# Attention probabilities times values as three rounded-half products in a fused decoder layer

## The chip, the cores and the metric

The kernel runs on one core of one Trainium2 chip. The metric is device time in microseconds (us) of one execution. The engines are TensorE (PE in the profile; PEld is its weight load), VectorE (DVE), ScalarE (ACT), GpSimd (POOL) and SyncE (SP), which issues the loads.

## What is computed

One layer of a hybrid decoder over 256 tokens of width 1024: a normalised input `h` goes through one wide input projection, three parallel branches (a matrix memory with four heads, a convolution module, native sparse attention) are computed from it, gated and merged, and an output projection follows. The change lies in the attention. Eight query heads share two groups of keys and values. For each head there are three softmaxes: over compressed keys (`kc`, 15 of them), over selected blocks, and over a window; at this length the last two cover all earlier tokens.

```python
s_c = jnp.einsum('bqgjd,bngd->bgjqn', qb, kc).astype(jnp.float32) * scale
p_c = masked_softmax(s_c, cmp_end[None, :] <= t[:, None])
o_c = jnp.einsum('bgjqn,bngd->bqgjd', p_c.astype(vc.dtype), vc)
...
o_s = jnp.einsum('bgjqk,bgqkd->bqgjd', p_s.astype(vs.dtype), vs)
...
o_w = jnp.einsum('bgjqk,bkgd->bqgjd', p_w.astype(vw.dtype), vw)
return gb[..., 0:1] * o_c + gb[..., 1:2] * o_s + gb[..., 2:3] * o_w
```

## The kernel before

All weights are streamed from HBM once, in tiles of 128 x 1024 (`w_raw`). Each is split in two: ACT casts it to the rounded format (`w_hi`, float32r), DVE subtracts to get the rest (`w_lo`), and a product with the likewise split `h` is the sum of three rounded-half matmuls (`feat`, L548; `group_feat`, L560; results in the PSUM tiles `ps_f`, and `ps_t` for token-major ones). One 128-wide output tile of `ps_f` is 24 matmuls of 256 columns.

A small planner, the `Loom` (L67 to L243), fixes the order of all instructions when the program is built. Every PE, ACT and DVE instruction goes through it; it estimates when each ends, and side work, written as generators that yield the time at which their operands should be due, is stepped between the matmuls of the projection (`weave`, L199, called in `feat`). Filler, the 31-tap convolution (`conv_gen`, L607, instructions named `acc`), is stepped whenever DVE looks idle. `need(task)` (L225) ends the waiting: it steps a generator to its end at once, and what is left of it is then issued in one block, with no projection matmul in between.

The attention is one such generator, `nsa_gen` (L898). It goes through four groups (two key groups g, two halves t of the tokens). For each: score products into `ps_s`, masks and maxima on DVE (`mx`), 12 exponentials on ACT over the tile `pm`, normalisation on DVE, and then per block of 128 keys: four transposes (`flip`) of `pm` into a PSUM bank `ps_p`, an ACT copy to `p_t`, and one f32 matmul of 512 columns with the values `vtok`, accumulated in `ps_o`. The compressed keys are one more block, of 16 rows, through `ptc` and `vcmp`. A group with t = 0 has two dense blocks, one with t = 1 has four; each has one compressed block. PSUM tag `sd` has three banks: one for `ps_o`, two for `ps_p`.

Around it, the program issues the projection groups in this order: four heads of `aq`, `ak`, `av`, `az`, `bz`; then `ao` (eight tiles, L1180), evacuated by ACT with a Sigmoid into `sz`; then `need(g_nsa)` (L1182), since the next group, `cz`, multiplies into the attention's output `oc`. Later three branch products follow (`ps_br`): c, then a, then b. Branch b needs the end of the convolution, a layer norm (`lnorm_gen`, L618: `ps_mu`, `ps_rc`), and `conf_tail` (L665): Silu on ACT, product with `zb` on DVE, split into `yb_hi` (ACT) and `yb_lo` (DVE). Its gates `gb` are projected just before, eight tiles, and then `need(g)` (L1245) forces what is left of `conf_tail`. Within a branch tile the products go pair by pair through the eight tiles of `y` in order.

Of the kernel before, what the change touches and what calls it, by code (L numbers as in the profile page):

```python
# [11 lines left out]
F32 = mybir.dt.float32  # L12
F32R = mybir.dt.float32r
# [51 lines left out]


class Loom:  # L67
    """Issues the instructions of every engine in the order of the trace and estimates when each one ends, so that
    side work can be woven between the matrix products once its operands are due."""

    HOP = {"pe": 250.0, "act": 130.0, "dve": 150.0, "dma": 0.0}
    OWN = {"pe": 0.0, "act": 140.0, "dve": 125.0, "dma": 0.0}
# [68 lines left out]
        return end  # L141

    def clocked(self, start, cost):
        """The tensor engine runs at half its clock after a window in which it was mostly idle."""
        w = int(start // 3413)
        while self.window < w:
            self.cold = self.busy < (0.9 if self.cold else 0.5) * 3413
            self.busy = 0.0
            self.window += 1
        self.busy += cost * (2 if self.cold else 1)  # L150
        return cost * (2 if self.cold else 1)
# [64 lines left out]
                self.tasks.remove(task)  # L216

    def spawn(self, gen, rank=2):
        """Ranks: 0 for what the tensor engine needs next, 1 for the chains of the heads, 2 for the rest."""
        task = [0.0, gen, False, rank]  # L220
        i = next((i for i, t in enumerate(self.tasks) if t[3] > rank or (t[3] == rank == 1)), len(self.tasks))
        self.tasks.insert(i, task)
        return task
# [5 lines left out]
        self.forcing -= 1  # L229

    def calm(self, engine, ap):
        """Waits while a run of exponentials keeps its table loaded."""
        yield self.until(engine, ap)
        while self.run and not self.forcing:
            yield self.now() + 300
# [8 lines left out]


class Line:
    """An engine whose instructions go through a Loom."""

    def __init__(self, loom, engine, name):
        self.loom, self.engine, self.name = loom, engine, name  # L250
# [7 lines left out]
def trunk(ctx: ExitStack, tc, xtok, crow, wada, wave0, wgrp, wmisc, w1, wbr, wout, par, vbias, out):  # L258
# [24 lines left out]
    def ringt(pool_, shape, name, tag, bufs, dt=F32):  # L283
        return loom.alloc(pool_.tile(shape, dt, name=name, tag=tag, bufs=bufs), tag, bufs)
# [431 lines left out]
    ckv = ckb[:, 0].rearrange("p (a b c) -> p a b c", a=2, b=2)  # L716
    kk = [const.tile([128, 528], F32, name=f"kk{g}") for g in range(2)]
    vtok = midt("vtok", [128, 2, 2, 256])
    vcmp = [const.tile([128, 128], F32, name=f"vcmp{g}") for g in range(2)]
    for g in range(2):  # L720
        pool.memset(vcmp[g], 0.0)

    def cmp_gen(j):
        for g in range(2):
            c = ckv[:, j, g, :]
            src = bass.AP(tensor=c.tensor, offset=c.offset, ap=[list(c.ap[0]), [1, 32], [16, 15]])
            dve.tensor_tensor(blk[:, :, 16 * g:16 * g + 15], src,
                              pc("pe", 32 * j, 32)[:, :, None].broadcast_to([128, 32, 15]), op=OP.add)
        yield from loom.slot("sd")
        ps = bank("ps_c1", "sd")  # L730

        def load(c):
            w = rawt([128, 8, 256], "w1_raw")
            loom.load(nc.sync, w, w1[4 * j + c])
            return w

        yield from raw_slot()
        nxt = load(0)
        for c in range(4):
            if c < 3:  # L740
                yield from raw_slot()
            w, nxt = nxt, load(c + 1) if c < 3 else None
            yield until("pe", w, blk)
            for e in range(8):
                q = e % 4
                mm(ps[32 * q:32 * q + 32, 0:256], blk[:, 8 * c + e, :], w[:, e], c == 0 and e < 4,
                   c == 3 and e >= 4, tile_position=(0, 32 * q), skip_group_check=True)
            raw_free(w)
        part = ringt(work, [128, 256], "part", "mu", 1)
        yield until("act", ps)  # L750
        act.copy(part, ps[:, 0:256])
        drop(ps)
        yield until("pe", part)
        yield from loom.slot("sd")
        ps = bank("ps_c2", "sd")
        for f in range(2):
            mm(ps[:, 32 * f:32 * f + 32], part[:, 128 * f:128 * f + 128], gather4, True, True)
        hid = work.tile([128, 64], F32, name="hid", tag="hid")
        yield until("act", ps)
        act.copy(hid, ps[:, 0:64])  # L760
        drop(ps)
        yield until("dve", hid)
        t = work.tile([128, 64], F32, name="gt", tag="gt")
        dve.tensor_tensor(t, hid, hid, op=OP.mult)
        dve.tensor_tensor(t, t, hid, op=OP.mult)
        dve.scalar_tensor_tensor(t, t, 0.044715, hid, op0=OP.mult, op1=OP.add)
        yield until("act", t)
        act.activation(t, t, AF.Tanh, scale=0.7978845608028654)
        yield until("dve", t)
        dve.tensor_scalar(t, t, 0.5, 0.5, op0=OP.mult, op1=OP.add)  # L770
        dve.tensor_tensor(hid, hid, t, op=OP.mult)
        yield until("pe", hid)
        w2 = [pc("w2", (2 * j + f) * 128, 128) for f in range(2)]
        if j == 0:
            yield from loom.slot("sd")
            ps = bank("ps_kc", "sd")
            for f in range(2):
                mm(ps[:, 0:32], w2[f], hid[:, 32 * f:32 * f + 32], f == 0, f == 1)
            yield until("act", ps)
            for g in range(2):  # L780
                act.copy(kk[g][:, 384:400], ps[:, 16 * g:16 * g + 16])
            drop(ps)
        else:
            for g in range(2):
                yield from loom.slot("sd")
                ps = bank("ps_vc", "sd")
                for f in range(2):
                    mm(ps[0:16, 0:128], hid[:, 32 * f + 16 * g:32 * f + 16 * g + 16], w2[f], f == 0, f == 1)
                yield until("act", ps)
                act.copy(vcmp[g][0:16, :], ps[0:16, 0:128])  # L790
                drop(ps)

    blk = ckb[:, 1].rearrange("p (a b) -> p a b", a=32)
# [104 lines left out]
    def nsa_gen(qs, oc, ptc):  # L898
        for g in range(2):
            for t in range(2):  # L900
# [80 lines left out]
                def flips(c, kind, kt):  # L981
# [4 lines left out]
                        flip(pt[0:w, 128 * j:128 * j + 128], pm[:, j, c:c + w])  # L986
                    yield until("act", pt)
                    if kind == 2:
                        act.copy(ptc[0:16, :], pt[0:16, :])
                        drop(pt)  # L990
                        return vcmp[g], ptc
                    p_t = ringt(work, [128, 512], "p_t", "p_t", 2)
                    act.copy(p_t, pt)
                    drop(pt)
                    return vtok[:, kt, kind, 128 * g:128 * g + 128], p_t

                ops = yield from flips(*blocks[0])
                for b in range(len(blocks)):
                    v, p_t = ops
                    if b + 1 < len(blocks):  # L1000
                        ops = yield from flips(*blocks[b + 1])
                    yield until("pe", p_t)
                    mm(po, v, p_t, b == 0, b == len(blocks) - 1)
                yield until("act", po)
                act.copy(oc[:, 4 * g:4 * g + 4, 128 * t:128 * t + 128], po.rearrange("p (j q) -> p j q", j=4))
                drop(po)
# [101 lines left out]
    for i in range(4):  # L1108
        group_feat("cq", i, evac_fn(lambda t: qs[:, t]))
    oc = bigt("oc")  # L1110
    ptc = const.tile([128, 512], F32, name="ptc")
    pool.memset(ptc, 0.0)

    def nsa_all():
        yield from loom.after(g_cmp, g_misc)
        yield from nsa_gen(qs, oc, ptc)

# [306 lines left out]
```

## Time and profile before

| | |
|---|---|
| runs (us) | 512.29, 512.80, 513.61; median 512.8 |
| profiled execution, span | 510.6 us; the median of the runs is 2.2 above it |
| PE busy | 502.0 us (98%), 3962 matmul instructions |
| PEld busy | 476.6 us (93%) |
| DVE busy | 431.5 us (85%), 894 instructions |
| ACT busy | 316.9 us (62%), 542 instructions, 27 of them table loads |
| DMA | 103.86 MB, mean 203 GB/s |
| chain that ended last | PE 96% |

The profiled execution has no time of its own beside its span, so the runs' median is what it is held against. A matmul's length in the time line includes its pipeline; the chain of waits shows how long each took from TensorE alone, from one start to the next. An f32 matmul shows as two instructions. On ACT a table load (ACT_TABLE_LOAD) precedes a function of another table than the last: Exp, Sigmoid, Silu and Sqrt each have their own here; copies, casts and Identity need none.

### The profile page before, as it was taken

What the parts mean: (1) busy time and instruction counts of PE and PEld (TensorE: products, weight loads), DVE (VectorE), ACT (ScalarE), POOL (GpSimd) and SP (SyncE); (2) the same over time, 40 slices, a digit from 0 to 9 for tenths busy, and PEclk for the clock granted to TensorE, in tenths of its full rate; (3) what the DMA queues carried; (4) which work ended last, traced back from release to release, by engine and by line L of the source; (5) the groups of instructions that cost most, each with busy time, mean ns of one, the idle gap of its engine ahead of it and who ended that gap; (6) DMA issues with size and microseconds to landing.
All of it is one profiled execution on the core that took longest, in us unless ns stands there. A gap on an engine that the chain in (4) does not pass through costs nothing.

```text
span 510.6 us, 10012 instructions
## 1 busy us (share of the span) xinstructions
PE 502.0 (98%) x3962; PEld 476.6 (93%) x3962; DVE 431.5 (85%) x894; ACT 316.9 (62%) x542; POOL 7.5 (1%) x42
## 2 busy tenths in 40 slices
PE   8999999999999999999999999999999999999994
PEld 6999999899889989979999989999999999999983
DVE  4998888899987998988989968999899997667755
ACT  5556666244566867779568995665534466975442
POOL 4000000000000000000000000000000000000000
PEclk9999999999999999999999999999999999999999
DMA  7999975884694424422523415544675664445502
GB/s 263 380 367 367 421 236 189 292 323 167 223 358 163 164 83 166 143 105 90 190 119 134 162 60 210 197 166 171 243 282 213 235 254 172 166 166 198 214 1 82
DMA packets 17617, 103.86 MB, mean 203 GB/s; under 512 B 2081, under 2 KB 2209, under 8 KB 7458
## 3 DMA queue, kind: packets, MB, share of 16 engines
q1 hardware_dynamic: 17570, 103.22, 55.0%
q8 instruction: 31, 0.51, 0.4%
q14 instruction: 16, 0.13, 0.1%
HBM read 102.16 MB, written 1.05 MB: 202 GB/s over the span
## 4 chain that ended last, share of the span: by engine, by line
PE 96%; DMA 1%; DVE 1%; ACT 0%; issue 0%; DVEq 0%; SPq 0%; ACTq 0%
PE ps_f L158 50%; PE ps_br L158 14%; PE w L158 9%; PE ps_t L158 7%; PE ps_out L158 4%; PE ps_o L158 3%; PE ps_s L158 2%; PE ps_c L158 2%; PE ps_p L158 1%; DMA x_sb<-in_xtok_dram 1%; PE ps_n L158 1%; PE ps_qk L158 1%; PE ps_heat L158 1%; PE ps_g L158 0%; PE ps_ht L158 0%; PE ps_mb L158 0%
## 5 line engine op out<-in xcount | busy, mean ns | idle before, releaser
L158 DVE TENSOR_TENSOR w_lo<-w_raw,w_hi 128x1024 fp32r<-128x1024 f32 x148 | 180.3, 1221 | 34.5 <-ACT w_hi L158 34.2
L158 ACT CAST w_hi<-w_raw 128x1024 fp32r<-128x1024 f32 x148 | 154.1, 1043 | 57.1 <-PE ps_br L158 16.9
L158 PE MATMUL ps_f<-h_hi,w_hi 128*128 128x256 f32 x704 | 177.4, 288 | 0.0
L158 PE MATMUL ps_f<-h_lo,w_hi 128*128 128x256 f32 x704 | 173.5, 283 | 0.0
L158 PEld LDWEIGHTS ps_f<-h_hi,w_hi 128*128 128x128 f32 x704 | 134.8, 192 | 2.2 <-issue 1.9
L158 PEld LDWEIGHTS ps_f<-h_lo,w_hi 128*128 128x128 f32 x704 | 134.9, 192 | 0.6 <-issue 0.2
L158 PE MATMUL ps_f<-h_hi,w_lo 128*128 128x256 f32 x704 | 102.7, 287 | 0.0
L158 DVE SCALAR_TENSOR_TENSOR acc<-u,p_sb,acc 128x226 f32<-128x226 f32 (+28 forms) x232 | 94.5, 463 | 8.6 <-ACT acc L158 8.4
L158 PEld LDWEIGHTS ps_f<-h_hi,w_lo 128*128 128x128 f32 x704 | 91.5, 192 | 2.4 <-issue 2.3
L158 ACT ACT_TABLE_LOAD x27 | 34.6, 1283 | 1.3 <-PEq L1416 0.8
L158 PE MATMUL w<-h_lo,w_hi 128*128 128x256 f32 x128 | 31.4, 283 | 0.0
L158 PE MATMUL w<-h_hi,w_lo 128*128 128x256 f32 x128 | 31.4, 283 | 0.0
L158 PE MATMUL ps_t<-w_hi,h_hi 128*128 128x256 f32 x96 | 29.6, 308 | 0.0
L158 DVE SCALAR_TENSOR_TENSOR a_raw<-a_raw,cb 128x1024 f32<-128x1024 f32 x24 | 28.5, 1220 | 0.0
L158 PE MATMUL ps_t<-w_hi,h_lo 128*128 128x256 f32 x96 | 27.1, 283 | 0.0
L158 PE MATMUL ps_t<-w_lo,h_hi 128*128 128x256 f32 x96 | 27.1, 282 | 0.0
L158 PEld LDWEIGHTS w<-h_hi,w_lo 128*128 128x128 f32 x128 | 24.6, 192 | 0.0
L158 PEld LDWEIGHTS w<-h_lo,w_hi 128*128 128x128 f32 x128 | 24.6, 192 | 0.0
L158 ACT ACTIVATE gs<-ps_f,p_sb 128x256 f32<-128x256 f32 x16 | 7.6, 476 | 25.5 <-PE ps_f L158 22.7
L158 PEld LDWEIGHTS ps_t<-w_hi,h_hi 128*128 128x128 f32 x96 | 18.3, 191 | 2.0 <-issue 1.7
L158 ACT ACTIVATE pm<-pm,mx 128x16 f32<-128x16 f32 (+2 forms) x48 | 19.1, 403 | 0.8 <-DVE mx L158 0.8
L158 PEld LDWEIGHTS ps_t<-w_lo,h_hi 128*128 128x128 f32 x96 | 18.3, 191 | 0.7 <-issue 0.5
(268 smaller groups left out, 777.0 us busy)
## 6 DMA issues: line engine op xcount, KB each, us to landing
w_raw<-in_wgrp_dram SPq DMA_DIRECT2D x50, 1024.0 KB, 4.9
w_raw<-in_wbr_dram SPq DMA_DIRECT2D x12, 1024.0 KB, 4.8
a_raw<-in_wada_dram SPq DMA_DIRECT2D x16, 512.0 KB, 7.3
w_raw<-in_wave_dram SPq DMA_DIRECT2D x16, 512.0 KB, 7.3
w_raw<-in_w_dram SPq DMA_DIRECT2D x8, 1024.0 KB, 4.9
a_raw<-in_wada_dram SPq DMA_DIRECT2D x4, 1024.0 KB, 5.2
w_raw<-in_wout_dram SPq DMA_DIRECT2D x4, 1024.0 KB, 4.9
x_sb<-in_xtok_dram SPq DMA_DIRECT2D x2, 512.0 KB, 4.7
```

Source lines behind the costliest of these rows:

```text
L158: inst = self.pin(fn(*args, **kw))
```

## The change

The values are split once (`vt_hi`, `vt_lo`, in `nsa_all`). Each dense block's transposed probabilities are split as they leave PSUM: ACT casts to `p_hi`, DVE subtracts to `p_lo`, and three rounded-half matmuls (hi x hi, lo x hi, hi x lo) replace the one f32 matmul. For the compressed keys the three terms are stacked on partitions 0, 32 and 64 of `ptc` and `vcmp`, which stay one matmul, in float32r: two ACT copies and one DVE subtraction each where one ACT copy was. The bank `ps_p` is now freed by DVE. A parameter of the builder shrinks a reserved space in SBUF, which gives the new tiles their room. The hunks that only remove docstrings are left out.

```diff
@@ -716,9 +716,10 @@
     ckv = ckb[:, 0].rearrange("p (a b c) -> p a b c", a=2, b=2)
     kk = [const.tile([128, 528], F32, name=f"kk{g}") for g in range(2)]
     vtok = midt("vtok", [128, 2, 2, 256])
-    vcmp = [const.tile([128, 128], F32, name=f"vcmp{g}") for g in range(2)]
+    vt_hi, vt_lo = [const.tile([128, 2, 2, 256], F32R, name=f"vt_{n}") for n in ("hi", "lo")]
+    vcmp = [const.tile([128, 128], F32R, name=f"vcmp{g}") for g in range(2)]
     for g in range(2):
-        pool.memset(vcmp[g], 0.0)
+        pool.memset(vcmp[g].bitcast(F32), 0.0)
 
     def cmp_gen(j):
         for g in range(2):
...
@@ -787,7 +788,10 @@
                 for f in range(2):
                     mm(ps[0:16, 0:128], hid[:, 32 * f + 16 * g:32 * f + 16 * g + 16], w2[f], f == 0, f == 1)
                 yield until("act", ps)
-                act.copy(vcmp[g][0:16, :], ps[0:16, 0:128])
+                for q in (0, 32):
+                    act.copy(vcmp[g][q:q + 16, :], ps[0:16, 0:128])
+                yield until("dve", vcmp[g])
+                dve.tensor_tensor(vcmp[g][64:80, :], ps[0:16, 0:128], vcmp[g][0:16, :], op=OP.subtract)
                 drop(ps)
 
     blk = ckb[:, 1].rearrange("p (a b) -> p a b", a=32)
...
@@ -986,21 +990,31 @@
                         flip(pt[0:w, 128 * j:128 * j + 128], pm[:, j, c:c + w])
                     yield until("act", pt)
                     if kind == 2:
-                        act.copy(ptc[0:16, :], pt[0:16, :])
+                        for q in (0, 64):
+                            act.copy(ptc[q:q + 16, :], pt[0:16, :])
+                        yield until("dve", ptc)
+                        dve.tensor_tensor(ptc[32:48, :], pt[0:16, :], ptc[0:16, :], op=OP.subtract)
                         drop(pt)
-                        return vcmp[g], ptc
-                    p_t = ringt(work, [128, 512], "p_t", "p_t", 2)
-                    act.copy(p_t, pt)
+                        return ((vcmp[g], ptc),)
+                    p_hi = ringt(work, [128, 512], "p_hi", "p_hi", 2, F32R)
+                    p_lo = ringt(work, [128, 512], "p_lo", "p_lo", 2, F32R)
+                    act.copy(p_hi, pt)
+                    yield until("dve", p_hi)
+                    dve.tensor_tensor(p_lo, pt, p_hi, op=OP.subtract)
                     drop(pt)
-                    return vtok[:, kt, kind, 128 * g:128 * g + 128], p_t
+                    v_hi, v_lo = [v[:, kt, kind, 128 * g:128 * g + 128] for v in (vt_hi, vt_lo)]
+                    return (v_hi, p_hi), (v_lo, p_hi), (v_hi, p_lo)
 
                 ops = yield from flips(*blocks[0])
                 for b in range(len(blocks)):
-                    v, p_t = ops
+                    pairs = ops
                     if b + 1 < len(blocks):
                         ops = yield from flips(*blocks[b + 1])
-                    yield until("pe", p_t)
-                    mm(po, v, p_t, b == 0, b == len(blocks) - 1)
+                    yield until("pe", *[p for _, p in pairs])
+                    for i, (v, p) in enumerate(pairs):
+                        mm(po, v, p, b == 0 and i == 0, b == len(blocks) - 1 and i == len(pairs) - 1)
+                    if len(pairs) > 1:
+                        drop(pairs[0][1], pairs[2][1])
                 yield until("act", po)
                 act.copy(oc[:, 4 * g:4 * g + 4, 128 * t:128 * t + 128], po.rearrange("p (j q) -> p j q", j=4))
                 drop(po)
...
@@ -1108,10 +1122,15 @@
     for i in range(4):
         group_feat("cq", i, evac_fn(lambda t: qs[:, t]))
     oc = bigt("oc")
-    ptc = const.tile([128, 512], F32, name="ptc")
-    pool.memset(ptc, 0.0)
+    ptc = const.tile([128, 512], F32R, name="ptc")
+    pool.memset(ptc.bitcast(F32), 0.0)
 
     def nsa_all():
+        for t in range(2):
+            yield until("act", vtok[:, t])
+            act.copy(vt_hi[:, t], vtok[:, t])
+            yield until("dve", vt_hi[:, t])
+            dve.tensor_tensor(vt_lo[:, t], vtok[:, t], vt_hi[:, t], op=OP.subtract)
         yield from loom.after(g_cmp, g_misc)
         yield from nsa_gen(qs, oc, ptc)
 
...
@@ -1413,7 +1432,7 @@
     from concourse.bass_utils import run_bass_kernel_spmd as _run
 
     arrays = pack(**inputs)
-    nc = _bacc.Bacc("TRN2", target_bir_lowering=False, num_devices=1)
+    nc = _bacc.Bacc("TRN2", target_bir_lowering=False, num_devices=1, dynamic_dma_scratch_size=1024)
     args = [nc.dram_tensor(f"in_{n}_dram", a.shape, mybir.dt.from_np(a.dtype), kind="ExternalInput").ap()
             for n, a in arrays.items()]
     args.append(nc.dram_tensor("out_0_dram", (S, D), F32, kind="ExternalOutput").ap())
```

The recorded order moves with it, since the planner's estimates move. On PE, the last attention group (g = 1, t = 1) before; `ps_f` here are `ao` tiles, `ps_n` is the matrix memory's:

```order
L158 MATMUL ps_f<-h_hi,w_hi 128x256
L158 MATMUL ps_f<-h_lo,w_hi 128x256
L158 MATMUL ps_o<-p_t,vtok 128x512
L158 MATMUL ps_p<-ident,pm 128x128 x4
L158 MATMUL ps_f<-h_hi,w_hi 128x256
L158 MATMUL ps_f<-h_lo,w_hi 128x256
L158 MATMUL ps_f<-h_hi,w_hi 128x256
L158 MATMUL ps_f<-h_lo,w_hi 128x256
L158 MATMUL ps_o<-p_t,vtok 128x512
L158 MATMUL ps_p<-ident,pm 128x128 x4
L158 MATMUL ps_f<-h_hi,w_hi 128x256
```

and now, from the end of the last `ao` tile:

```order
L158 MATMUL ps_f<-h_lo,w_hi 128x256
L158 MATMUL ps_f<-h_hi,w_lo 128x256 x8
L158 MATMUL ps_p<-ident,pm 128x128 x8
L158 MATMUL ps_o<-p_hi,vt_hi 128x512
L158 MATMUL ps_o<-p_hi,vt_lo 128x512
L158 MATMUL ps_o<-p_lo,vt_hi 128x512
L158 MATMUL ps_p<-ident,pm 128x128 x4
L158 MATMUL ps_o<-p_hi,vt_hi 128x512
L158 MATMUL ps_o<-p_hi,vt_lo 128x512
L158 MATMUL ps_o<-p_lo,vt_hi 128x512
L158 MATMUL ps_p<-ident,pm 128x128 x4
L158 MATMUL ps_o<-p_hi,vt_hi 128x512
```

The flips and products, which stood among `ps_f` matmuls, stand in one block behind the last `ao` tile. On ACT, the exponentials of that group (`pm`) before, among evacuations with Identity (`ga`, `zb`):

```order
L158 ACTIVATE ga<-ps_f,p_sb 128x256
L158 CAST w_hi<-w_raw 128x1024
L158 ACTIVATE pm,sm<-pm,mx 128x16
L158 ACTIVATE pm,sm<-pm,mx 128x256
L158 ACTIVATE pm,sm<-pm,mx 128x2x128
L158 ACTIVATE ga<-ps_f,p_sb 128x256
L158 CAST w_hi<-w_raw 128x1024
L158 ACTIVATE pm,sm<-pm,mx 128x16
L158 ACTIVATE pm,sm<-pm,mx 128x256
L158 ACTIVATE pm,sm<-pm,mx 128x2x128
L158 ACTIVATE zb<-ps_f,p_sb 128x256
L158 CAST w_hi<-w_raw 128x1024
```

and now, from the evacuation of the fifth `ao` tile (tiles are counted from 0, so the first `sz` shown below is tile 4's):

```order
L158 ACT_TABLE_LOAD
L158 ACTIVATE sz<-ps_f,p_sb 128x256
L158 CAST w_hi<-w_raw 128x1024
L158 ACT_TABLE_LOAD
L158 ACTIVATE pm,sm<-pm,mx 128x16
L158 ACT_TABLE_LOAD
L158 ACTIVATE sz<-ps_f,p_sb 128x256
L158 CAST w_hi<-w_raw 128x1024
L158 ACT_TABLE_LOAD
L158 ACTIVATE pm,sm<-pm,mx 128x256
L158 ACT_TABLE_LOAD
L158 ACTIVATE sz<-ps_f,p_sb 128x256
```

Each exponential now stands between two table loads, as the evacuations `sz` are Sigmoids; ahead of these rows stand tile 3's evacuation, a cast, a load and three exponentials, and behind them a cast, tile 7's evacuation, a load, seven exponentials and the casts `p_hi`. On ACT ahead of branch b, `conf_tail` before:

```order
L158 ACTIVATE gb<-ps_f,p_sb 128x256
L158 CAST w_hi<-w_raw 128x1024
L158 ACTIVATE gb<-ps_f,p_sb 128x256
L158 CAST w_hi<-w_raw 128x1024
L158 CAST yb_hi<-zb 128x512
L158 ACT_TABLE_LOAD
L158 ACTIVATE u<-u,p_sb 128x256 x4
L158 ACT_TABLE_LOAD
L158 ACTIVATE gb<-ps_f,p_sb 128x256
L158 CAST w_hi<-w_raw 128x1024
L158 CAST yb_hi<-zb 128x512
L158 ACTIVATE gb<-ps_f,p_sb 128x256
```

and now:

```order
L158 ACTIVATE gb<-ps_f,p_sb 128x256
L158 CAST w_hi<-w_raw 128x1024
L158 ACTIVATE gb<-ps_f,p_sb 128x256
L158 ACT_TABLE_LOAD
L158 ACTIVATE u<-u,p_sb 128x256 x4
L158 CAST yb_hi<-zb 128x512 x2
L158 ACTIVATE u<-u,p_sb 128x256 x4
L158 CAST yb_hi<-zb 128x512 x2
L158 CAST w_hi<-w_raw 128x1024 x2
```

The Silus (`u`) and casts `yb_hi`, which were spread over the `gb` tiles, now all follow the last `gb` evacuation.

## Rows read from the trace of the kernel before

**Rows 1.** The page, header of the profiled execution.

```profile
span 510.6 us, 10012 instructions
```

**Rows 2.** Who waited for whom, TensorE (engine, line, releaser: total, times, longest).

```profile
PE ps_heat L158 <- POOL ones L296: 1.1, 1, 1.1
PE ps_x L158 <- ACT x_sb L158: 0.7, 1, 0.7
```

**Rows 3.** The chain that ended last (start us, length us, engine, what, line, instructions).

```profile
298.42 0.44 PE ps_p L158 x4
...
302.57 0.86 PE ps_o L158 x2
303.43 43.19 PE ps_f L158 x360
...
481.96 21.80 PE ps_out L158 x96
503.85 0.70 ACT sqo L158 x2
```

**Rows 4.** Instructions grouped by shape, ACT then DVE (count | busy us, mean ns).

```profile
L158 ACT COPY p_t<-ps_p 128x512 f32<-128x512 f32 x12 | 6.8, 586 | 2.0 <-PE ps_p L158 2.0
...
L158 ACT COPY ptc<-ps_p 16x512 f32<-16x512 f32 x4 | 2.3, 574 | 2.8 <-PE ps_p L158 2.8
...
L158 DVE TENSOR_TENSOR yc_lo<-oc,yc_hi 128x512 fp32r<-128x512 f32 x4 | 2.7, 685 | 0.0
```

**Rows 5.** Time line of ACT, 270 to 277 us (start us, length us, what).

```profile
270.12 1.28 ACT L158 ACT_TABLE_LOAD   x1
271.41 0.31 ACT L158 ACTIVATE pm<-pm,mx 128x16 f32<-128x16 f32 x1
...
273.15 0.50 ACT L158 ACTIVATE pm<-pm,mx 128x256 f32<-128x256 f32 x1
...
273.65 0.29 ACT L158 ACTIVATE pm<-pm,mx 128x16 f32<-128x16 f32 x1
...
273.94 0.50 ACT L158 ACTIVATE pm<-pm,mx 128x256 f32<-128x256 f32 x1
...
274.93 0.46 ACT L158 ACTIVATE ga<-ps_f,p_sb 128x256 f32<-128x256 f32 x1
275.29 1.04 ACT L158 CAST w_hi<-w_raw 128x1024 fp32r<-128x1024 f32 x1
276.22 0.31 ACT L158 ACTIVATE pm<-pm,mx 128x16 f32<-128x16 f32 x1
```

**Rows 6.** Time line of DVE, 280 to 284 us.

```profile
280.77 0.22 DVE L158 TENSOR_TENSOR pm<-pm,keep 128x64 f32<-128x64 f32 x1
...
283.30 1.22 DVE L158 TENSOR_TENSOR w_lo<-w_raw,w_hi 128x1024 fp32r<-128x1024 f32 x1
```

**Rows 7.** Time line of ACT, 434 to 438 us.

```profile
434.45 2.08 ACT L158 ACTIVATE u<-u,p_sb 128x256 f32<-128x256 f32 x4
...
437.37 0.62 ACT L158 CAST yb_hi<-zb 128x512 fp32r<-128x512 f32 x1
```

**Rows 8.** Time line of DVE, 438 to 440 us.

```profile
438.64 0.69 DVE L158 TENSOR_TENSOR yb_lo<-zb,yb_hi 128x512 fp32r<-128x512 f32 x1
439.24 0.69 DVE L158 TENSOR_TENSOR zb<-zb,u 128x512 f32<-128x512 f32 x1
```

**Rows 9.** Time line of TensorE, the first 11 us.

```profile
1.05 4.21 PE L158 MATMUL ps_heat<-ones 128*128 128x128 f32 x18 [1.05 <-POOL ones L296]
5.06 2.97 PE L158 MATMUL ps_cb<-c_sb,ones 128*128 128x512 f32 x4
7.86 1.05 PE L158 MATMUL ps_x<-ident,x_sb 128*128 128x128 f32 x8
8.75 1.95 PE L158 MATMUL ps_heat<-ones 128*128 128x128 f32 x16
```

**Rows 10.** Busy time by window; the number before the DMA share is the granted clock.

```profile
505.00:510.60 5.60, 0.00 (x0) 0.00 (x0) 2.32 (x5) 0.20 (x1) 0.00 (x0) 0.86 0.36 140
```

## Prediction

> **What bounds the kernel now.** I read the header, then who waited for whom on TensorE, then the chain that ended last, then the time lines of ScalarE (ACT) and VectorE (DVE) where the attention runs. The span is 510.6 us [rows 1]. TensorE waits for another engine for 1.8 us in all of it, both times in the first 12 us [rows 2], and the chain runs along TensorE without a break from there to its last matmul at 503.9 us [rows 3]. So every microsecond of TensorE work is a microsecond of the span, and the two engines that feed it are hidden, but only because the order written by the Loom puts enough `ps_f` matmuls between a request and its use. The order is fixed when the program is built: a later operand stops TensorE, and nothing behind it can overtake. So the change has two parts: the work it takes off TensorE, and what the new order leaves between requests and uses.
>
> **A, TensorE's own work.** One f32 matmul of 512 columns takes two instructions and 0.86 us, four flips 0.44, one 256-column rounded-half matmul 43.19/360 = 0.12, and one of 512 columns 21.80/96 = 0.227 [rows 3]. Before there are 16 f32 products on `ps_o` (12 blocks of 128 keys, 4 of compressed keys): 16 x 0.86 = 13.8 us. After there are 12 x 3 + 4 = 40 rounded-half ones: 40 x 0.227 = 9.1. The stacked compressed product is still one matmul, so its three terms are free on TensorE. **A = -4.7 us**, all on the path.
>
> **Side work.** DVE gains 12 subtractions `p_lo`, 4 on `ptc`, 2 for `vt_lo` of about 0.69 and 2 small ones: some 13 us; ACT gains 4 copies of `ptc` of 0.57, 2 casts `vt_hi` of about 0.62 and 2 small ones: some 4 us [rows 4, 7]. I cost these at nothing by themselves, since the convolution (`acc`) is filler that the Loom puts off. What they displace is the point: the convolution and the attention chain both come later. Counting input-projection matmuls (`ps_f`, `ps_t`) ahead of the first flips of the four attention groups, the order has 800, 1036, 1228, 1464 before and 892, 1152, 1396, 1632 now. Each block also passes ACT and then DVE before its product, where it passed ACT alone. Before, the last group ended well inside the eight `ao` tiles; now its flips stand at exactly the matmul after the last `ao` tile, where `need(g_nsa)` forces whatever is left, with no `ps_f` between. That is the first stop.
>
> **B, stop at `need(g_nsa)`.** The exponentials of the last group now fall among the `ao` evacuations, which are Sigmoids, so ACT reloads its table at every turn. From the end of `ao` tile 3 to the last exponential the new order gives ACT 7 table loads, 5 evacuations, 4 casts `w_hi`, and 12 exponentials (4 of each of three pieces). By the distances of starts [rows 5]: a load 271.41 - 270.12 = 1.29, a 256-wide exponential with its accumulator 0.50, a 16-wide one 0.29, an evacuation 0.36 to 0.37, a cast 0.93. Sum: 9.0 + 1.85 + 3.75 + 4 x (0.50 + 0.50 + 0.29) = 19.8 us. TensorE meanwhile has tiles 4 to 7, 96 x 0.12 = 11.5 us, so the exponentials end 8.3 us after it has run out. DVE then normalises up to the first scaled piece, 280.77 to 283.30 = 2.5 us [rows 6]. Then the forced blocks: flips, cast `p_hi` 0.59, `p_lo` 0.69, three products, with two banks to alternate; stepping through the five blocks, with the two `ptc` copies and their subtraction last, gives 8.0 us, of which 5.15 is TensorE's own work (20 flips 2.2, 13 products 2.95), already in the total. **B = 8.3 + 2.5 + 2.85 = 13.7 us.**
>
> By the Trainium skill ("ScalarE: Activation LUTs", What ACT_TABLE_LOAD costs) a switch is the load of about 1.28 us and a drain of about 1.38. The load agrees with the page's row of 1.28; but the exponential starts 1.29 after the load did [rows 5], so no such drain shows here. By the page B would be some 9.7 us longer, by the rows it is as above, and I go by the rows.
>
> **C, stop at the third branch.** The convolution ends later too: the matmuls between `ps_mu` and the first product of branch b fall from 416 to 164, and between the last `ps_rc` and that product from 256 to 40. Before, Silu, product and split of `yb` were spread over the `gb` tiles; now all of them stand behind the last `gb` evacuation, forced. From the last `gb` matmul: evacuation and load 0.17 + 0.37 + 1.29 = 1.8; four Silus 2.0 [rows 7]; in the queues behind them two casts of 0.62 with DVE's `zb` 0.69 and `yb_lo` 0.69 in turn [rows 7, 8], so that the second four Silus run from about 6.3 to 8.3; then cast, `yb_lo`, `zb`, cast, `yb_lo`, about 3.4: 11.7 us to the last pair. TensorE does the 12 matmuls of the first three pairs in between (1.4). **C = 10.3 us.**
>
> **D, the clock.** TensorE's last matmul ends at 503.9 us, and the mean granted clock over the window from 505 on is 0.86 of full speed [rows 3, 10]. With the two levels 2.4 and 1.2 GHz that is a fall at about 505 + 5.6 x 0.72 = 509.0, some 5 us after TensorE went idle. At the kernel's start nine heating matmuls take 4.21 us, later eight take 1.95, 0.47 against 0.24 each, and the two `ps_cb` take 2.80 where 1.72 would do [rows 9]: half speed up to about 7.2 us, which costs some 3.1 us. TensorE is idle 10.8 us before the forced flips and about 5 us before the first `yb` pair. Nothing in this trace shows a fall in mid-kernel, so I bound it: 0 if neither gap is long enough, 2 x 3.1 + 2.5 (the flips and products of B at half speed) = 8.7 if both are. The first gap is twice the 5 us, the second just at it: **D = 5 us**, nearer the upper end. By the Trainium skill ("TensorE: Matmul & The Clock Gate", Part 1) the throttled state is the default and only activity lifts it, which would put D at the upper end.
>
> **Sum.** 510.6 - 4.7 + 13.7 + 10.3 + 5.0 = 534.9 us of span. The median of the three runs, 512.8, stands 2.2 above the profiled span, and I add that: **537 us**, 4.7% slower.
>
> **Rivals.**
> *The stops are hidden, and the saving stands* (508 us, faster). It needs ACT's 19.8 us list, DVE's 2.5 and the first block to fit in the 108 matmuls, 12.9 us, that the order leaves between the last scores and the forced flips, and the `yb` chain to fit in the 40 matmuls (4.8 us) left to it. It decides for a gain from the point where B, C and D together are under 4.7. For it: the Loom costs every instruction it places, and before it left no wait. Against: it estimates, and forcing overrides its estimates.
> *Only B happens* (about 525: 512.8 - 4.7 + 13.7 + 3), if idle DVE during B lets the `yb` chain catch up. Against: DVE's queue is in order and holds nothing of the convolution inside B.
> *The other eight dense blocks wait as well.* Each p_lo that comes 0.8 us late, the wait of a block in B's stepping, adds up to 6.4: about 543. Against: 16 to 40 `ps_f` matmuls mostly stand between their flips and products.
> *A drain at each switch* (the page above): 8 switches in B and C, 11 us more: 548. The rows speak against it.
> *The products don't run as rounded halves.* At 0.86 each, 40 would cost 34 us, 25 more. But the `ps_out` rows are such matmuls of 512 columns at 0.227.
>
> **Numbers.** Chances: the forecast, both stops with D between 0 and 8.7, 0.79 (529 to 542); hidden stops 0.06; only B 0.05; further waits 0.06; drain 0.03; no halves 0.01. The range 527 to 547 leaves out the hidden stops, most of B alone, the drain and the last. A measurement of this kernel can tell about 0.3% (1.5 us) from no change. Faster 0.06, same 0.01 (stops that just eat the saving), slower 0.93.
>
> **What would show it.** TensorE waiting some 11 us before a `ps_p`, released by DVE's `pm`, with the wait's end shared by a row of ACT table loads just ahead; short waits before `ps_o` in the same place; a wait of about 10 us in pieces before the first `ps_br<-yb`; a granted clock under 1.00 in both places; the `ps_o` group at 40 instructions of 0.39 us. I am wrong if TensorE's waits still total under 5 us, if ACT reaches the last exponential before the last `ao` tile ends, or if the loss sits in the first 270 us.

## The result, and the profile after

The changed kernel takes 542.94 us (median of 4 runs, 542.34 to 544.57); the kernel before takes 512.71 beside it (4 runs, 512.29 to 513.61). The ratio is 1.0595, with a 95% interval of 1.0579 to 1.0611: slower by 30.2 us where 24.2 were forecast. The profiled execution took 544.57 us, of which 542.9 are its span; against [rows 1] that is 32.3 us more. I account for the spans.

The page after: span, busy time, and the granted clock in 40 slices.

```profile
span 542.9 us, 10064 instructions
...
PE 510.0 (94%) x3970; PEld 485.3 (89%) x3970; DVE 445.3 (82%) x914; ACT 321.6 (59%) x550; POOL 7.5 (1%) x42
...
PEclk9999999999999999999998977999999999977998
```

TensorE, DVE and ACT each have a lower share of the span than before, though DVE and ACT were given work: the time is in waiting. Who waited for whom, TensorE (total, times, longest), which answers to [rows 2]:

```profile
PE ps_p L158 <- DVE pm L158: 11.5, 1, 11.5
PE ps_o L158 <- DVE ptc L158: 5.8, 4, 3.8
PE ps_br L158 <- ACT yb_hi L158: 5.7, 4, 4.4
```

The first and the third row are the forecast stops B and C. The second holds one that was not forecast.

**Stop B.** TensorE's time line, from the last `ao` tile to the first tile behind the attention:

```profile
312.79 1.12 PE L158 MATMUL ps_f<-h_hi,w_lo 128*128 128x256 f32 x8
325.37 1.94 PE L158 MATMUL ps_p<-ident,pm 128*128 128x128 f32 x8 [11.46 <-DVE pm L158]
...
334.67 0.50 PE L158 MATMUL ps_o<-ptc,vcmp 128*128 128x512 f32 x1 [1.20 <-DVE ptc L158]
335.00 0.28 PE L158 MATMUL ps_f<-h_hi,w_hi 128*128 128x256 f32 x1
```

The `ao` tiles are issued by 312.79 + 8 x 0.12 = 313.75, the next tile starts at 335.00: 21.25 us, less 5.15 of its own flips and products, so **B is 16.1**. ACT's time line in the same stretch, and the chain's row for the last exponentials:

```profile
309.29 1.28 ACT L158 ACT_TABLE_LOAD   x1
310.58 0.31 ACT L158 ACTIVATE pm<-pm,mx 128x16 f32<-128x16 f32 x1
310.80 0.19 ACT L158 ACTIVATION_READ_ACCUMULATOR pm<-pm,mx 128x1 f32 x1
311.00 1.28 ACT L158 ACT_TABLE_LOAD   x1
312.30 0.47 ACT L158 ACTIVATE sz<-ps_f,p_sb 128x256 f32<-128x256 f32 x1
```

```profile
320.00 3.15 ACT pm L158 x14
```

One exponential, a load, one Sigmoid, a load: the list of the forecast. It ends at 323.15, 9.4 us behind the last tile (forecast 8.3). A load starts 1.29 us ahead of the instruction behind it, and directly behind the one before it (310.80 + 0.19, then 311.00). The Trainium skill ("ScalarE: Activation LUTs", What ACT_TABLE_LOAD costs) adds a drain of about 1.38 us to each switch; by these starts there is none here.

**Stop C.** The chain that ended last, from the last `gb` evacuation (start, length):

```profile
478.22 0.47 ACT gb L158
...
489.81 24.04 PE ps_br L158 x179
513.85 21.80 PE ps_out L158 x96
```

From 478.03, where the last `gb` matmul was issued (its row of eight starts at 477.07), to 489.81 the chain is ACT and DVE: 11.78 us (forecast 11.7). Behind it 179 matmuls take 24.04 where 179 x 0.12 = 21.5 would do. **C with its clock is 12.8**: 35.8 us from 478.03 to the first `ps_out`, less 192 x 0.12.

**The clock** (window, its length, PE busy, granted clock, DMA share, GB/s):

```profile
290.00:295.00 5.00, 5.00 (x27) 0.66 0.00 0
...
318.00:324.00 6.00, 0.00 (x0) 0.50 0.00 0
324.00:330.00 6.00, 4.63 (x17) 0.50 0.00 0
...
485.00:490.00 5.00, 3.56 (x10) 0.50 0.00 0
490.00:495.00 5.00, 5.00 (x24) 0.50 0.00 0
```

In both stops TensorE stands idle, falls to its lower level, 1.2 GHz, and stays there for the first work behind the wait. It is also at 0.66 from 290 to 295, and that belongs to the stop I had not seen.

**The third stop.** ACT, DVE and TensorE around 289 us, in the group g = 1, t = 0:

```profile
280.91 1.16 ACT L158 CAST ptc<-ps_p 16x512 fp32r<-16x512 f32 x2
282.09 1.28 ACT L158 ACT_TABLE_LOAD   x1
...
284.55 1.28 ACT L158 ACT_TABLE_LOAD   x1
...
287.21 0.37 ACT L158 COPY num<-ps_n 128x256 f32<-128x256 f32 x1
```

```profile
287.62 0.43 DVE L158 BATCH_NORM_STATS2 st<-ps_n 128x6 f32<-128x256 f32 x1 [3.11 <-ACT num L158]
...
288.28 0.68 DVE L158 TENSOR_TENSOR ptc<-ps_p,ptc 16x512 fp32r<-16x512 f32 x1
```

```profile
289.11 0.47 PE L158 MATMUL ps_o<-ptc,vcmp 128*128 128x512 f32 x1 [3.77 <-DVE ptc L158]
```

The subtraction that completes `ptc` had its operands at 280.91 + 1.16 = 282.07. It ran at 288.28, because DVE's queue is in order and ahead of it stood a BN_STATS that waited for ACT's `num`, behind two table loads. TensorE waited 3.77 us, and its clock was 0.66 over the next 5: 1.7 more, **5.5 in all**.

| part | forecast | measured, us of span |
|---|---|---|
| A, products (worked out under the run spaced) | -4.7 | at best -4.2 |
| B with its clock | 13.7 + 2.5 | 16.1 |
| C with its clock | 10.3 + 2.5 | 12.8 |
| third stop with its clock | - | 5.5 |
| other waits on `ptc` (0.33, 0.55) | - | 0.9 |
| later start (first `ps_m` at 74.34; 73.64 before) | - | 0.7 |
| sum | 24.3 | 31.8 of 32.3 |

### The profile page after: what moved, and what is told of

Its sections match the earlier page's. It is cut to its first block, busy times and chain, and to the rows that moved or that the text cites. A ratio compares the mean times of both kernels' runs of the same rounds, so it can differ in the third digit from the quotient of the medians.

```text
span 542.9 us, 10064 instructions
## 1 busy us (share of the span) xinstructions
PE 510.0 (94%) x3970; PEld 485.3 (89%) x3970; DVE 445.3 (82%) x914; ACT 321.6 (59%) x550; POOL 7.5 (1%) x42
## 4 chain that ended last, share of the span: by engine, by line
PE 84%; ACT 8%; DVE 3%; DMA 3%; issue 1%; DVEq 0%; SPq 0%; ACTq 0%
PE ps_f L158 44%; PE ps_br L158 13%; PE ps_t L158 6%; PE w L158 6%; PE ps_out L158 4%; ACT L158 2%; PE ps_s L158 2%; PE ps_c L158 2%; PE ps_o L158 2%; PE ps_p L158 2%; DMA w_raw<-in_wave_dram 1%; ACT w_hi L158 1%; DMA x_sb<-in_xtok_dram 1%; PE ps_qk L158 1%; ACT pm L158 1%
## 5 line engine op out<-in xcount | busy, mean ns | idle before, releaser
L158 PE MATMUL ps_t<-w_hi,h_hi 128*128 128x256 f32 x96 | 27.5, 287 | 0.0
L158 PE MATMUL ps_br<-yb_hi,w_hi 128*128 128x256 f32 x64 | 18.9, 324 | 5.7 <-ACT yb_hi L158 5.7
L158 PE MATMUL ps_p<-ident,pm 128*128 128x128 f32 (+1 forms) x64 | 11.0, 305 | 11.5 <-DVE pm L158 11.5
L158 PEld LDWEIGHTS ps_p<-ident,pm 128*128 128x128 f32 (+1 forms) x64 | 8.5, 148 | 13.4 <-issue 12.0
```

The source lines that it names most:

```text
L158: inst = self.pin(fn(*args, **kw))
```

## The experiments

Two theories stood against each other: the loss is the **order** that the Loom now writes, or it is the **work** added on DVE and ACT. The first two runs take one of them each.

**held: the work without the order.** The added instructions are issued but not charged to the Loom, and the first of three products is charged at the f32 price, so that all the instructions of before keep their places.

```diff
+                    loom.ghost = True
                     dve.tensor_tensor(p_lo, pt, p_hi, op=OP.subtract)
+                    loom.ghost = False
...
+                        loom.ghost, loom.price = i > 0, 512 * 4 / 2.4 + 2
                         mm(po, v, p, b == 0 and i == 0, b == len(blocks) - 1 and i == len(pairs) - 1)
```

> The change in full, but the Loom is not charged for the added casts and subtractions, and of the three products it is charged for one at the old f32 price; so every instruction that was there before keeps its place, and each added one stands right behind the one it belongs to. Theory (the whole loss is the new order; the work itself is hidden): TensorE's saving of 4.7 stands alone, 512.7 - 4.7 = 508.0 us, between 507 and 510; no wait of TensorE over 1 us after the first 12 us. Rival 1 (the added 13 us of DVE and 4 us of ACT cost time where they stand): 513 or more. Rival 2 (the products save nothing in place): 512.7.

Measured: 519.06 us beside 512.11, ratio 1.0123 (1.0093 to 1.0152). That is the rival's side, and my theory in its plain form fell: in its old places the work costs 11 us more than the 508 expected. TensorE's waits in this run:

```profile
PE ps_o L160 <- DVE ptc L160: 4.2, 3, 2.3
PE ps_s L160 <- DVE mx L160: 1.7, 1, 1.7
...
PE ps_o L160 <- DVE p_lo L160: 0.8, 2, 0.4
PE ps_n L160 <- DVE wt L160: 0.7, 1, 0.7
```

The old order left room for one ACT copy between flips and product; now an ACT and a DVE step have to fit. DVE's queue in the longest wait:

```profile
257.56 2.35 DVE L160 SCALAR_TENSOR_TENSOR acc<-u,p_sb,acc 128x237 f32<-128x237 f32 x6
259.94 0.68 DVE L160 TENSOR_TENSOR ptc<-ps_p,ptc 16x512 fp32r<-16x512 f32 x1
```

ACT's two copies were done at 258.36; the subtraction stood behind six pieces of the convolution. The waits add up to 7.4 us, and behind the longest the granted clock was 0.66 from 260 to 265, 1.7 us more. So most of the 11 us is late operands. The two long stops, however, are gone.

**phantom: the order without the work.** The kernel before, f32 products and all; only the Loom is charged as if the added instructions were there.

```diff
                     act.copy(p_t, pt)
+                    yield until("dve", p_t)
+                    loom.charge("dve", 68 + 512 / 0.96, [p_t], [pt, p_t])
```

> The kernel before, with its f32 products and none of the added instructions, but the Loom is charged for them as if they were there; so the instructions that both kernels have stand in the changed kernel's order. Theory (the loss is the order): the two long stops are there, 542.9 + 4.7 for the f32 products, less 5.5 for the wait on the subtraction of ptc near 289 us and its clock loss (without a subtraction there, only the ACT copy, done at 282, is waited for), less 1 to 4 for the p_lo that the forced blocks no longer wait for: 537 to 542 us. Rival (the loss is the added work): 512 to 518.

Measured: 539.07, ratio 1.0516 (1.0492 to 1.0539), as the theory had it. TensorE's waits:

```profile
PE ps_p L159 <- DVE pm L159: 11.4, 1, 11.4
PE ps_br L159 <- ACT yb_hi L159: 5.7, 4, 4.4
```

Without one added instruction both stops are there at full size, and the waits on `ptc` are not. Up to the end of the forced blocks this run has the changed kernel's order, instruction for instruction on all three engines. Behind them, against what was expected, pieces of the convolution and some other instructions stand elsewhere. So B is the order alone, C is made by an order like the changed kernel's without the added work, and the third stop needs the added subtraction.

**early_sub: the third stop alone.** The subtraction of `ptc` is issued directly behind its two copies; the Loom is charged where it was before, so that nothing else moves.

```diff
+                        loom.ghost = True
+                        dve.tensor_tensor(ptc[32:48, :], pt[0:16, :], ptc[0:16, :], op=OP.subtract)
+                        loom.ghost = False
                         yield until("dve", ptc)
-                        dve.tensor_tensor(ptc[32:48, :], pt[0:16, :], ptc[0:16, :], op=OP.subtract)
+                        loom.charge("dve", 68 + 512 / 0.96, [ptc[32:48, :]], [pt[0:16, :], ptc[0:16, :]])
```

> The changed kernel; the subtraction that fills the middle part of ptc stands on DVE directly behind the two ACT copies it reads, up to eight instructions earlier than before (three of the four move), and nothing else moves on any engine. Theory (the stop near 289 us, which the prediction did not have, is this subtraction standing behind a BN_STATS that waits for ACT behind two table loads, while its own operands were ready at 282.07): the stop of 3.8 us and the fall of the clock behind it (1.6 by the heated run) vanish: 542.9 - 5.4 = 537.5 us, between 536 and 539; both long stops stay as they are. Rival (the stop has another cause that is late too, ACT's next casts or the matrix memory's operands): 541 to 544.

Measured: 539.53, ratio 1.0534 (1.0514 to 1.0554), 3.1 us below the changed kernel by the ratios: the theory's side, but 2 short of its point and half a microsecond outside its range. The waits show why:

```profile
PE ps_o L159 <- DVE ptc L159: 1.9, 3, 1.2
PE ps_n L159 <- DVE wt L159: 1.4, 1, 1.4
```

```profile
282.08 0.68 DVE L159 TENSOR_TENSOR ptc<-ps_p,ptc 16x512 fp32r<-16x512 f32 x1 [1.45 <-ACT ptc L159]
```

The wait of 3.8 is gone (the longest left on `ptc`, 1.2, is the one inside B), and with it the fall of the clock (1.00 from 290 to 295). A wait of 1.4 on `wt`, an operand of the matrix memory, is new, and the edit made it: the subtraction now stands at the head of DVE's queue for 1.45 us until ACT has written `ptc`, and `wt`, which stands behind it, comes later. In the changed kernel nothing waited for `wt`, so this is not the rival's other cause.

**noswitch: the cause of stop B.** The `ao` tiles are evacuated by Identity, while the Loom is told Sigmoid.

```diff
+        loom.table_as = AF.Sigmoid
-        act.activation(s, ps, AF.Sigmoid, bias=b)
+        act.activation(s, ps, AF.Identity, bias=b)
+        loom.table_as = None
```

> The changed kernel with the ao tiles evacuated by Identity in the place of Sigmoid (the sigmoid is left out), in the unchanged order: 7 table loads fall away, 9.0 us of ACT. Theory (the first stop is ACT's list of loads, evacuations, casts and exponentials against 11.5 us of ao matmuls): the list is 10.8 us, the exponentials end with the last ao tile, the wait before the forced flips falls from 11.5 to about 3, the clock hardly falls: 542.9 - 8.5 - 2 = 532.5 us, between 531 and 535. Rival (the stop is set elsewhere, by DVE's normalisation or late scores): a wait of 8 us or more stays, 540 to 543.

Measured: 534.73, ratio 1.0435 (1.0415 to 1.0454), inside the theory's range, though not all of it by the theory's way. The wait before the forced flips:

```profile
PE ps_p L159 <- DVE pm L159: 5.8, 1, 5.8
```

It halves, from 11.5, but not to 3: the 14 exponential rows of the end still stand behind the last tile. The table loads are some 6 of stop B's 16 us (from the last tile to the next, 14.9 us here against 21.4 on the chain, with the same own work). The clock still fell (0.72 from 312 to 318), which the theory did not expect. And only six of the seven loads stood in B; the seventh stood in the third stop, whose wait fell from 3.8 to 2.4. The Trainium skill ("ScalarE: Activation LUTs", Rules for kernel authors) says to group by table set and do all of one before switching. The 8 us for 7 loads are the most that grouping these Sigmoids and exponentials could give here, since this run leaves the Sigmoid out altogether.

**heat: the clock.** Heating matmuls in the three idle stretches, not charged to the Loom (each between the `ghost` lines of held).

```diff
+    heat(44)
     need(g_nsa)
...
+            heat(18)
         for g in before[i]:
...
                     yield until("pe", *[p for _, p in pairs])
+                    if g == 1 and t == 0 and len(pairs) == 1:
+                        heat(14)
```

> The changed kernel with three runs of small heating matmuls put into TensorE's three idle stretches, in the unchanged order: 44 (10.3 us at full clock) ahead of the forced attention blocks, 18 ahead of branch b, 14 ahead of the late compressed product near 289 us. Theory (a clock that fell in the stops is part of the loss): no wait gets shorter, but the granted clock stays at 1.00, which gives back about 2.5 in the forced blocks, 2.5 in branch b and 1.8 behind 289 us: 542.9 - 6.8 = 536 us, between 534.5 and 538. Rival (the clock does not matter, TensorE is paced by ACT and DVE there anyway): 543.

Measured: 539.97, ratio 1.0533 (1.0509 to 1.0556): 3.2 us below the changed kernel by the ratios, not 6.8. Behind 289 us the gain came nearly as expected (1.6 for 1.8, from the late product to the flips' wait). In the two stops it did not, and the granted clock shows where:

```profile
318.00:324.00 6.00, 4.37 (x40) 1.00 0.00 0
324.00:330.00 6.00, 5.76 (x29) 0.72 0.00 0
...
485.00:490.00 5.00, 4.28 (x16) 0.54 0.00 0
```

With most of the idle stretches filled (1.6 us of the first was left, and up to 1.1 at a time of the second), the clock held until 324 and until 485, and then fell inside the forced work, whose matmuls stand apart waiting for ACT and DVE. The forced blocks went from 9.6 to 8.9 us, branch b hardly moved. Whether the clock would have held with nothing left idle, no run shows. The Trainium skill ("TensorE: Matmul & The Clock Gate", Part 1) calls the throttled state the default, which activity lifts; the rows agree as far as they go: 1.00 while the heating ran, and less once the matmuls stood apart.

**slack0: stop C alone.** `SLACK`, the margin ahead of a TensorE matmul, from 250 to 0.

> The changed kernel with one number of the Loom changed: no safety margin (0.25 us before) between the time an operand is due on TensorE and its matmul. The attention then ends inside the ao tiles (last product at 1572 of 1632 projection matmuls), but no matmul lies between the last ps_rc and branch b. Theory (the two long stops are independent, each with its own price): the first stop is gone, the second stays with 11 to 14 us, waits on ptc of 2 to 4 us: 512.1 - 4.7 + 11..14 + 2..4 = 520 to 526 us. Rival (the second stop is only what the first has delayed): 508 to 513.

Measured: 524.79, ratio 1.0245 (1.0231 to 1.0259), inside the theory's range.

```profile
PE ps_br L158 <- ACT yb_hi L158: 5.8, 4, 4.6
PE ps_o L158 <- DVE ptc L158: 2.4, 3, 1.2
```

No wait on `pm`, and the waits of C as in the changed kernel. Stop C does not need stop B, and B lies 160 us ahead of it.

**cmp_only and dense_only: each part of the change alone**, with the hunks of the other left out.

> The stacking of the compressed keys alone; the dense blocks keep their f32 product and one copy. It saves 4 x 0.63 = 2.5 us of products. Its last flips stand at 1616 to 1632, not in one block, 220 matmuls behind the last scores, and 352 matmuls lie between the last ps_rc and branch b. Theory (a part costs what its order leaves uncovered, not its work): no long stop, 509.6 + short waits of 1 to 5 us: 510.5 to 515. Rival (each part costs its share of the added work, 3 of 13 us of DVE): 519.

> The split of the dense blocks alone; the compressed keys keep their f32 product and one copy. It saves 12 x (0.86 - 0.68) = 2.2 us of products. Its last flips are forced into one block behind the ao tiles, but 264 matmuls behind the last scores (108 in the changed kernel), and 220 matmuls lie between the last ps_rc and branch b. Theory (a forced block alone costs little; the stop comes from operands that are late at that point): 509.9 + 3 for the block's own chain + short waits of up to 4: 511 to 517 us. Rival (each part costs its share of the added work, 10 of 13 us of DVE): 535.

Measured: 519.77, ratio 1.0143 (1.0129 to 1.0157), and 517.76, ratio 1.0108 (1.0094 to 1.0122). The first misses my range and hits the rival's number; the second lies just above my range, 17 below the rival. Shares of the work can't explain both: the part with the less work costs the more, and 7.3 + 5.3 is far from 30. In dense_only the last flips are forced into one block as well, and TensorE does not wait for `pm` at all: being forced makes no long stop where the operands are there in time. In cmp_only the largest loss is not on anything that the change added (TensorE, then DVE):

```profile
301.55 1.40 PE L158 MATMUL ps_f<-h_hi,w_lo 128*128 128x256 f32 x8 [4.06 <-DVE w_lo L158]
```

```profile
299.02 0.95 DVE L158 SCALAR_TENSOR_TENSOR acc<-u,p_sb,acc 128x226 f32<-128x226 f32 x2 [4.03 <-ACT acc L158]
...
300.27 1.22 DVE L158 TENSOR_TENSOR w_lo<-w_raw,w_hi 128x1024 fp32r<-128x1024 f32 x1
```

A piece of the convolution, filler, stood at the head of DVE's queue waiting for ACT, and the weights that TensorE needed stood behind it.

**room3000, seen_room3000, b_room3000: another order by one number.** `ROOM`, how far ahead side work may be queued, from 900 to 3000. In the second run the Loom is also shown all of `ptc`. It keys what it knows of a tile by offsets (`span`, `when`), and those of partitions 32 and 64 lie outside what it looks up for the whole tile, so the compressed product is placed by the first copy alone.

```diff
-                    yield until("pe", *[p for _, p in pairs])
+                    yield until("pe", *([p for _, p in pairs] if len(pairs) > 1 else [ptc[q:q + 16, :] for q in (0, 32, 64)]))
```

> The changed kernel with one number of the Loom changed: side work may be queued up to 3.0 us ahead on ACT and DVE in the place of 0.9. All added work is there and charged; the last flips now stand at 1484 to 1540 projection matmuls, spread, and 248 matmuls lie between the last ps_rc and branch b. Theory (the two long stops come from forcing, and only from it): no stop over 4 us, the saving less the short waits on ptc that the held run showed (4 to 9 us): 512 to 518 us. Rival (the added work costs some 20 us or more in whatever order): 528 or more.

> As the run with 3.0 us, and in addition the Loom is told of all three writes of ptc (partitions 0, 32 and 64), where it takes the first copy alone for the whole tile; the compressed product then stands where the subtraction is due. Theory (the waits on ptc come from this blind spot, those of the changed kernel and of the held run alike): waits of TensorE on ptc under 1 us in all, 508 to 513 us. Rival (DVE's real lateness, not the Loom's view, makes them): waits on ptc of 3 us or more, 512 to 518.

> The kernel before with the same 3.0 us in the Loom and no other edit: the control for the two runs with this number. TensorE waits for nothing in the kernel before, so a better order has nothing to give: 511.5 to 514 us. If it is faster by 2 us or more, what the two runs gain over the kernel before is not the products'.

Measured: 524.07, 1.0231 (1.0215 to 1.0246); 521.75, 1.0191 (1.0176 to 1.0206); and the control 523.58, 1.0228 (1.0211 to 1.0245). All three miss their ranges, and the control is the lesson: this number alone costs the kernel before 11 us, and at this number the change costs nothing. The waits, of the first, the second and the control:

```profile
PE ps_o L158 <- DVE ptc L158: 3.8, 2, 3.5
PE ps_f L158 <- DVE w_lo L158: 3.1, 2, 1.8
```

```profile
PE ps_f L158 <- DVE w_lo L158: 7.0, 2, 5.8
```

```profile
PE ps_f L158 <- DVE w_lo L158: 6.9, 4, 2.5
```

More side work queued ahead makes the weights late. Shown all of `ptc`, the Loom leaves no wait on it, which agrees with the blind spot. But the order moved with that too, so this run does not show it by itself, and a wait on `w_lo` of 5.8 took its place.

**spaced: the work with a little room.** As held, but the products are charged as they are, and the Loom waits longer ahead of each block's products. (The expectation's "7 us" of the held run are those over the kernel before; over its expectation it was 11.)

```diff
-                    yield until("pe", *[p for _, p in pairs])
+                    yield until("pe", *[p for _, p in pairs]) + (1200 if len(pairs) == 1 else 300)
```

> The change in full. The added casts and subtractions are issued right behind the instruction they belong to and not charged to the Loom; the products are charged as they are; and the Loom waits 0.3 us longer before a dense block's products and 1.2 us longer before a compressed one. The last flips stand at 1508 to 1532 projection matmuls, 164 matmuls behind the last scores, and 196 lie between the last ps_rc and branch b. Theory (the held run's 7 us over its expectation are its waits on ptc, p_lo and mx, because the old order leaves an added ACT and DVE step no room, and a little room is all that is missing): 512.1 - 4.7 + at most 2 for short waits = 507.4 to 509.5 us; waits of TensorE behind the first 12 us under 2 us in all. Rival (the added 17 us of ACT and DVE work cost time wherever they stand): 514 or more.

Measured: 511.95 us (11 runs) beside 512.44 (15 runs), ratio 0.9993 (0.9984 to 1.0002): no difference that can be told, 31 us below the changed kernel. It lies between the two sides, some 2 above the theory's range and 2 below the rival. The waits are nearly gone:

```profile
PE ps_o L160 <- DVE ptc L160: 2.0, 3, 1.3
```

This is what the products give when little is lost to the order. A block's three products (TensorE's time line):

```profile
296.18 0.39 PE L160 MATMUL ps_o<-p_hi,vt_hi 128*128 128x512 f32 x1
...
296.87 0.60 PE L160 MATMUL ps_p<-ident,pm 128*128 128x128 f32 x4
```

296.87 - 296.18 = 0.69 us for three, where one f32 product took 0.86 [rows 3]; a compressed one takes 0.23 to 0.34. So A is at best 13.8 - 12 x 0.70 - 4 x 0.3 = 4.2 us. In this run it is less: by the starts in TensorE's time line all products take 10.2 us against 13.7 before, 3.5 less, as three of the dense blocks took 0.84 to 0.93. The three waits on `ptc` cost 2.5, by the distance of starts less the 0.12 that the matmul ahead takes, each 0.16 more than its idle time, and one on `yb_lo` 0.2. That leaves 0.8, and the spans differ by 0.6. No run beat the kernel before.

## Why the prediction was right, and where it was off

The sign, the two places and the range held, for the reasons given: the order is fixed at build time, forcing overrides the Loom's estimates, and what is late stops TensorE. Step by step:

- *What bounds the kernel.* Right: TensorE had no wait [rows 2], so each wait shows in full.
- *A.* Right in kind; 0.5 to 1.2 too large, since a compressed product takes 0.23 to 0.34 and not 0.227, and three dense blocks of spaced took 0.84 to 0.93 and not 0.68.
- *"Side work. I cost these at nothing by themselves."* **This is the step that failed.** In the old places (held) the same work costs 11 us over the saving, and in the new order the subtraction of `ptc` made the third stop, 5.5 of the 8.0 us by which the forecast span was short. I looked for late operands only where a block was forced. The compressed block is always the last of its group, has no flips of a next block between it and the products before, and hangs on a DVE step that the Loom can't see; a look at DVE's queue ahead of each of the four subtractions would have shown the BN_STATS. Early_sub takes this wait away, and phantom does not have it.
- *B.* Right to 0.1 us with its clock, but by errors that cancel: 0.8 us too little for ACT and DVE before the flips (11.6 against 10.8), 0.9 too much for the blocks (9.6 against 8.0 + 2.5). That the sum came out so close is luck. Phantom shows the stop to be the order's, noswitch that the table loads are some 6 us of it.
- *C.* Right to 0.1 us; slack0 shows it alone.
- *D.* In C about 2.5 us are there by the rows. In B the clock's share is not told apart from the waits inside the forced blocks, and the 1.7 behind 289 were not in the forecast. What heating got back is 3.2, half of that at the third stop and 0.8 in B: the clock falls again inside sparse work, which my picture of a fall in the idle stretch and a recovery behind it did not have.
- *Rivals.* In the changed kernel no dense block waited on `p_lo`. The drain is not in the rows. The third stop is the rival "further waits" in kind, at the compressed blocks and not at the dense ones, for which I had priced it. The space in SBUF that the change takes from the builder is no cause: phantom does not have that hunk and is slow, spaced has it and is not.

What stays open: what the clock costs in B, and why the Loom's order is good for the kernel before and so easily worse; that it moves with any charge is shown (ratios from 1.00 to 1.06 over nine orders), the rule behind it is not.

## What to carry to other kernels

Where a program's own planner fixes the order at build time, a change of a few microseconds of side work is a change of the whole order: compare the recorded orders first, and look for work that is forced in a block while its operands are late. Then walk each in-order queue ahead of every instruction that something new waits for, and ask what stands in front of it and what that waits for, table loads above all. To learn what an edit is worth, run it in the old order and the new order without it; here those were +7 and +27 us, and the edit with a little room was worth nothing measurable.

## What the runs showed of the hardware

Heating did not carry over into sparse work: with TensorE kept busy through 10 us of the 11.5 us wait, the granted clock stood at 1.00 until 324 us and at 0.72 over the next 6, in which the flips and products stood apart. And one instruction of filler at the head of DVE's queue, waiting 4.03 us for ACT behind casts, an evacuation, an exponential and a table load, turned into a TensorE wait of 4.06 us for weights that share no data with it, through the order of the queue alone.
